# A two-layer hybrid trunk on one core: the scheduler plays the program through with another simulator of instruction times

## The chip, the core and the metric

The kernel runs on one core of a Trainium2 chip. The metric is the time of one execution in device microseconds (us); lower is better. TensorE (PE, with its weight load PEld), VectorE (DVE), ScalarE (ACT), GpSimd (POOL) and SyncE (SP, which issues the transfers here) each run their own stream of instructions in the order in which the program was laid down, and wait for one another on semaphores.

## The reference

512 prompt tokens and 8 x 4 decode tokens (N = 544) go through two layers, an mLSTM mixer and a gated DeltaNet (GDN) mixer, each followed by an MLP; every sub-layer ends in a LayerNorm. All is float32, D = 1024.

```python
for layer in range(DEPTH):                      # 0: mLSTM, 1: gated DeltaNet
    y, state = mixer[layer](x, state)           # projections, scan over the tokens, gate, output projection
    x = layer_norm(ALPHA * x + y)
    x = layer_norm(ALPHA * x + square(relu(x @ w1)) @ w2)

def step(S, xc):                                # the GDN scan, chunk after chunk
    u_c, w_c, attn_c, qg_c, kdec_c, gL_c = xc
    v_new = u_c - w_c @ S
    o = qg_c @ S + attn_c @ v_new
    S = gL_c * S + kdec_c.T @ v_new
    return S, o                                 # then o is normalised per head
```

The mLSTM scan is of the same kind (a state that each chunk reads and renews). The outputs are the tokens and all the states.

## The kernel before

**The products.** Activations stand as feature tiles, 128 features by 544 tokens, cut into two halves of 272. A float32 product is made of three matmuls of rounded parts (`mm3`, L157: hi hi, lo hi, hi lo). `load_w` (L143) brings a tile of weights in through SP's queue, ACT makes its high part (L110) and DVE its low part (L111). The L157 matmuls are most of PE's work; those of the projections depend on nothing but weights and the layer's input, so they can be done while PE would otherwise wait for something else. This is called filler below.

**The steps.** The mixers are written as steps in a fixed program order, `ORDER_A` for mLSTM and `ORDER` for GDN:

```python
ORDER_A = "p0 s0 p1 s1 d0 y0 p2 s2 p3 s3 w0 d1 y1 w1"
ORDER = "p0 a0 p1 i0 a1 d0 s0 p2 i1 u0 a2 s1 y0 p3 i2 a3 d1 s2 p4 i3 u1 s3 a4 w0 y1 p5 i4 p6 a5 d2 s4 w1 u2 i5 s5 y2 a6 p7 i6 a7 d3 s6 w2 u3 i7 s7 y3 w3"
```

`p` projects a unit (a quarter of mLSTM, an eighth of GDN), `a` prepares a GDN unit, `i` inverts its triangular blocks, `s` scans it over four chunks, `d` does the decode steps of a group, `u` renews the decode states, `y` projects and applies the output gate, `w` is the output projection. The steps `a`, `i`, `s`, `d` and `u` are written under `tc.high_priority(offset=HP)` with HP = 400 (L830, L833, L1374): the scheduler takes a ready instruction of these before a ready one of the rest.

**A scan is a chain.** One chunk of a GDN scan goes from engine to engine: PE L1180 (the state times k and q) → DVE L1183 (rhs, twice) → PE L1192 → DVE L1194 (vd) and ACT L1196 (vn) → PE L1200, with DVE L1203 renewing the state → PE L1210 → DVE L1212 (oi) → ACT L1152 twice, L1153, L1154 (the heads' norm) → DVE L1156 (go_on) → PE L1169 (transposes) → ACT L1171. Then the next chunk's L1180. The decode step of mLSTM goes PE L782 → ACT and DVE L672 to L683 (the norm, one small instruction after the other) → PE L785, then PE L795 against DVE L796. The update of the GDN decode states is PE L1327, three matmuls, against DVE L1332, four instructions, eight times a group. These chains work in PSUM tiles of tag s (`pm_s`, two banks), the projections in tag g (`pg_t`, three banks); one bank set can be used while the other waits.

**What fixes the order.** The program is written inside `tile.TileContext` (L1526). It collects the instructions, and its scheduler lays down one order per engine: it plays the program through with a model of how long each instruction takes, and whenever an engine is free there it gives it the ready instruction of the highest priority. Program order and `high_priority` give the priority; the model of times decides what is ready when. On the chip the order is fixed: an instruction that has to wait holds up everything behind it on its engine.

By time the stages lie so: mLSTM mixer to 284 us, MLP to 665, GDN mixer to 1440, MLP and the last LayerNorm to the end.

Of the kernel before, what the change touches and what calls it, by code (L numbers as in the profile page):

```python
# [16 lines left out]
P = 128  # L17
# [53 lines left out]
def hybrid_kernel(  # L71
# [46 lines left out]
    def gtile():  # L118
        """A bank for a product; the mlp has seven in turn."""
        tag = "g"  # L120
        if once:
            tag = once.pop(0)
        elif wide:
            wide.append(wide.pop(0))
            tag = wide[-1]
        if tag != "g":
            return mtile(tag)[:, :HN]
        return pg.tile([P, 512], F32, tag="g", name="pg_t", bufs=BANKS[0])[:, :HN]
# [7 lines left out]
    wn, wx = [0], [None]  # L136

    def load_w(src, alloc=None):
        """A tile of weights as hi and lo float32r parts."""
# [12 lines left out]
    def mm3(ps, h, wh, wl, xh, xl, first=True, last=True):  # L152
        """ps += W^T x for one half of the tokens: hi hi + hi lo + lo hi."""
# [11 lines left out]
    def gate_w(i, wt=None):  # L165
        """The gates' weights, side by side: hi in columns 0-47, lo in 64-111."""
# [9 lines left out]
    def gate_mm(ps, wt, h, k):  # L176
        """One half of the tokens: W_hi x on rows 0-47, W_lo x_hi on rows 64-111."""
# [4 lines left out]
    def projs(srcs, alloc=None, skip=2):  # L182
        """Feature tiles of the projections of X, the first half of the tokens first; alloc: of the weights after skip."""
# [46 lines left out]
    with tc.tile_pool(name="tmpc", bufs=1) as tp:  # L230
# [4 lines left out]
        # keep where t > s (strict) / t >= s  # L235
# [4 lines left out]
        # block of four: col // 4 == row // 4  # L240
# [5 lines left out]
        # rowm[r, j] = (r // 4 == j)  # L246
# [6 lines left out]
        # bmask[r, b] = (r % 32 // 4 == b)  # L253
# [3 lines left out]
        # bm16[r, j] = (r // 16 == j)  # L257
        G.affine_select(bm16, o1[:, :8], pattern=[[-16, 8]], compare_op=ALU.is_ge, fill=0.0, base=0, channel_multiplier=1)
        G.affine_select(bm16, bm16, pattern=[[16, 8]], compare_op=ALU.is_ge, fill=0.0, base=15, channel_multiplier=-1)
        # upper[r] = -(r // 16 is even)  # L260
        V.reduce_sum(upper, bm16[:, 0::2], axis=mybir.AxisListType.X, negate=True)
        # dmask[r, h] = (r % 32 == h)
# [6 lines left out]
        # hm[r, q, h] = (r == 64 q + h) + (r == 64 q + 32 + h)  # L269
        for q in range(2):  # L270
            V.tensor_tensor(hmr[:, q], ident[:, 64 * q:64 * q + HV], ident[:, 64 * q + 32:64 * q + 32 + HV], op=ALU.add)
        # lvl[i]: upper off-diagonal blocks at block size 2**i: same 2s block, row in its first half, col in its second
# [11 lines left out]
    class LayerNorm:  # L284
        """Post-norm of the residual in XR, by halves of the tokens; the sums are of x - c, c a mean of 128 features
        taken one stage before the residual is complete."""
# [72 lines left out]
    def out_proj(src, yh, yl, first, ln=None):  # L359
        """src [4, 128, 2, 4, 128]: output tiles in pairs, four contraction tiles each; ln: of the next stage."""  # L360
# [10 lines left out]
    def out_proj_ln(src, yh, yl, ln, alloc, nxt=None):  # L371
        """The last stage, one half of the tokens after the other, each followed by its layer norm."""
# [8 lines left out]
        for h in range(2):  # L381
            pss = []
            for j in range(KD):
                if j == 0 and h == 0:
                    # before the last contraction tile is there
# [68 lines left out]
    def softplus(tile, out, x, r):  # L454
        """out = softplus(x) on partitions r (log1p with its first-order correction)."""
# [6 lines left out]
        # u - (w - 1)  # L462
# [5 lines left out]
    def sigmoid_chain(t, src):  # L468
        """t = sigmoid(src), through exp and ln only; src None: t holds it, clamped."""
# [10 lines left out]
    def selector(pool, g, n):  # L480
        """float32r lhsT that pick head 4g + h's row (hi and lo) for n columns each."""
# [4 lines left out]
    def expand_rows(pool, src, g):  # L486
        """[rows, 32 sample columns] of the stack -> [rows, (head of four, 32)], each head's rows only."""
# [9 lines left out]
    def expand_rows_r(pool, src, g, n):  # L497
        """The same of n hi/lo pairs of row blocks, kept in float32r."""
# [10 lines left out]
    # ================= layer 0: mLSTM =================  # L509
    ln = LayerNorm(0)  # L510
    with tc.tile_pool(name="mc", bufs=1, reuse_waits="tile") as mc, ExitStack() as mx:
# [88 lines left out]
        # what is written late comes where the gates were, what the layer norm reads next to it  # L600
# [13 lines left out]
        def project(u):  # L614
            """q, k, v of a pair of heads (features of the two on partitions 0-63 and 64-127)."""
# [33 lines left out]
            # exp(b_t - m_t + i_s - b_s), s on partitions  # L649
# [880 lines left out]
```

## Time and profile before

| what | before |
|---|---|
| runs | 1839.61, 1844.43, 1849.94 us |
| median | 1844.43 us |
| profiled execution, its own time | 1839.61 us |
| its span, first to last instruction | 1839.6 us |
| instructions | 33677 |
| PE busy | 97% of the span |
| PE's weight load busy | 94% |
| DVE, ACT, POOL busy | 58%, 46%, 1% |
| mean granted TensorE clock | 0.979 of full |

The profiled execution is the fastest of the three runs. A PE that is 97% busy leaves 55 us of the span in which it runs nothing. The granted clock has two levels, 2.4 GHz (1.00) and 1.2 GHz (half); a mean of 0.979 over the span says that in a small part of it the clock was at the lower one.

### The profile page before, as it was taken

The numbers are of one execution on the slowest core, as the hardware profiler recorded it, in microseconds if no ns is written. First come the engines' busy times: TensorE is split into PE (matmuls) and PEld (weight loads), VectorE is DVE, ScalarE is ACT, GpSimd is POOL, SyncE is SP. The second block draws the span as 40 slices with busy tenths as digits, with TensorE's granted clock in tenths as the row PEclk, the third lists the DMA queues.
The fourth block names the chain that finished last, engine by engine and source line by source line (L and its number), as shares of the span: only waits on it lengthen the run. The fifth ranks groups of instructions, "written<-read, shape, count | busy, mean of one in ns | idle before, by whom it ended". The sixth has DMA issues, their size and how long they took to land.

```text
span 1839.6 us, 33677 instructions
## 1 busy us (share of the span) xinstructions
PE 1784.3 (97%) x13620; PEld 1720.3 (94%) x13620; DVE 1070.4 (58%) x2622; ACT 844.7 (46%) x1922; POOL 13.7 (1%) x32
## 2 busy tenths in 40 slices
PE   7999999999999999899999999999999999999997
PEld 6999998999999998898999999899998999999996
DVE  6464767432344377767748857875668643234436
ACT  6444356331243147665647456646446532124314
POOL 2000000000000000000000000000000000000000
PEclk9999998999999999899979999999899999999999
DMA  4132122223223222224221413331232232322311
GB/s 159 58 104 67 67 92 92 77 85 92 86 87 105 83 70 62 66 65 135 68 75 55 150 57 111 108 93 59 87 108 84 81 92 82 92 90 84 112 61 50
DMA packets 84284, 158.75 MB, mean 86 GB/s; under 512 B 37536, under 2 KB 41504, under 8 KB 83616
## 3 DMA queue, kind: packets, MB, share of 16 engines
q1 hardware_dynamic: 84128, 156.60, 27.8%
q8 instruction: 107, 1.75, 0.4%
q14 instruction: 49, 0.40, 0.1%
HBM read 140.51 MB, written 16.06 MB: 85 GB/s over the span
## 4 chain that ended last, share of the span: by engine, by line
PE 83%; DVE 8%; ACT 6%; DMA 2%; issue 1%; SPq 0%; ACTq 0%; DVEq 0%
PE pg_t L157 39%; PE pm_s L157 12%; PE pm_a L157 12%; PE pm_a L1110 4%; PE pm_s L1282 2%; PE pm_s L1180 1%; DVE lnt L341 1%; ACT wh L110 1%; DVE lnt L342 1%; PE pm_s L1200 1%; PE pm_s L1327 1%; PE pm_a L1050 1%; PE pm_s L1192 1%; PE pm_s L1210 1%; DVE wl L111 1%
## 5 line engine op out<-in xcount | busy, mean ns | idle before, releaser
L111 DVE TENSOR_TENSOR wl<-wraw,wh 128x1024 fp32r<-128x1024 f32 x200 | 244.7, 1223 | 370.0 <-ACT wh L110 369.7
L157 PE MATMUL pg_t<-XH,wh 128*128 128x272 f32 x1480 | 442.8, 299 | 9.1 <-ACT XH L110 8.2
L157 PE MATMUL pg_t<-XH,wl 128*128 128x272 f32 x1480 | 438.6, 297 | 0.5 <-DVE wl L111 0.5
L157 PE MATMUL pg_t<-XL,wh 128*128 128x272 f32 x1480 | 438.0, 296 | 0.0
L110 ACT CAST wh<-wraw 128x1024 fp32r<-128x1024 f32 (+1 forms) x201 | 210.3, 1046 | 476.1 <-PE pg_t L157 230.0
L157 PEld LDWEIGHTS pg_t<-XH,wh 128*128 128x128 f32 x1480 | 284.1, 192 | 12.3 <-ACT XH L110 8.2
L157 PEld LDWEIGHTS pg_t<-XL,wh 128*128 128x128 f32 x1480 | 284.0, 192 | 1.2
L157 PEld LDWEIGHTS pg_t<-XH,wl 128*128 128x128 f32 x1480 | 283.3, 192 | 1.7 <-DVE wl L111 0.7
L157 PE MATMUL pg_t<-h,wh 128*128 128x272 f32 x672 | 129.1, 289 | 0.0
L157 PEld LDWEIGHTS pg_t<-h,wh 128*128 128x128 f32 x672 | 105.6, 188 | 0.3
L157 PE MATMUL pg_t<-h,wl 128*128 128x272 f32 x336 | 96.8, 288 | 0.0
L157 PE MATMUL pm_a<-h,wh 128*128 128x272 f32 x496 | 95.3, 288 | 0.0
L157 PE MATMUL pm_s<-h,wh 128*128 128x272 f32 x496 | 95.0, 288 | 0.0
L157 PE MATMUL pm_s<-XH,wh 128*128 128x272 f32 x288 | 84.4, 293 | 0.0
L157 PE MATMUL pm_s<-XH,wl 128*128 128x272 f32 x288 | 83.9, 291 | 0.0
L157 PE MATMUL pm_s<-XL,wh 128*128 128x272 f32 x288 | 83.8, 291 | 0.0
L157 PE MATMUL pm_a<-XL,wh 128*128 128x272 f32 x280 | 82.0, 293 | 1.0 <-DVE XL L353 0.8
L157 PE MATMUL pm_a<-XH,wh 128*128 128x272 f32 x280 | 82.2, 293 | 0.0
L157 PE MATMUL pm_a<-XH,wl 128*128 128x272 f32 x280 | 81.0, 289 | 0.0
L357 DVE SCALAR_TENSOR_TENSOR XR<-XR,pg_t 128x272 f32<-128x272 f32 x118 | 50.7, 432 | 48.4 <-PE pg_t L157 48.2
L959 DVE SCALAR_TENSOR_TENSOR acc<-pre,cst,acc 128x568 f32<-128x568 f32 x96 | 77.0, 802 | 2.8 <-ACT acc L957 2.4
L157 PEld LDWEIGHTS pm_s<-h,wh 128*128 128x128 f32 x496 | 77.9, 188 | 0.2
(559 smaller groups left out, 3997.7 us busy)
## 6 DMA issues: line engine op xcount, KB each, us to landing
wraw<-in_w SPq DMA_DIRECT2D x64, 512.0 KB, 3.6
wraw<-in_wb SPq DMA_DIRECT2D x48, 512.0 KB, 3.7
wraw<-in_w2a SPq DMA_DIRECT2D x32, 512.0 KB, 3.6
sst<-in_s SPq DMA_DIRECT2D x64, 256.0 KB, 3.4
wraw<-in_wa SPq DMA_DIRECT2D x24, 512.0 KB, 3.7
wraw<-in_w2b SPq DMA_DIRECT2D x24, 512.0 KB, 3.6
out_ss<-sst SPq DMA_DIRECT2D x32, 256.0 KB, 2.7
wraw<-in_wbo SPq DMA_DIRECT2D x16, 512.0 KB, 3.5
```

The source lines that it names most:

```text
L110: S.copy(hi, src)
L111: V.tensor_tensor(lo, src, r32(hi), op=ALU.subtract)
L157: T.matmul(ps, lhsT=wt[:, k, :], rhs=xt[k][:, HS[h]], start=first and k == 0 and q == 0, stop=last and k == n - 1 and q == 2,)
L341: V.tensor_tensor(t, x, rs, op=ALU.mult)
L342: V.tensor_tensor(t, t, mu, op=ALU.subtract)
L357: V.scalar_tensor_tensor(x, x, ALPHA if first else 1.0, ps, op0=ALU.mult, op1=ALU.add)
L959: V.scalar_tensor_tensor(acc, pre[:, q:q + WC], cw[q], acc, op0=ALU.mult, op1=ALU.add)
L1050: T.matmul(pk[:, q * 256:(q + 1) * 256], lhsT=kq[:, 0, c0:c0 + P], rhs=kq[:, :, c0:c0 + P], start=True, stop=True)
L1110: T.matmul(ps[:, c], lhsT=left[:, c], rhs=right[:, c], start=True, stop=True)
L1180: T.matmul(pks[:, w], lhsT=kq[:, w, cc], rhs=St, start=True, stop=True)
L1192: T.matmul(pv[:, j], lhsT=X[:, 4 * (ch // 2) + 2 * j + ch % 2], rhs=rhs[:, j] if ch else vtok[:, j, 0], start=True, stop=True)
L1282: T.matmul(pkq[:, bb], lhsT=ts[bb // 4][:, bb % 4], rhs=kqf[:, :, o:o + 4], start=True, stop=True)
```

## The change

The context is opened with the flag that makes the scheduler play the program through with the simulator of instruction times instead of its default model. Nothing else that has an effect is changed: the other lines of the diff take comments and docstrings out.

```diff
-    with tile.TileContext(nc) as tc:
+    with tile.TileContext(nc, schedule_with_timeline_sim=True) as tc:
         hybrid_kernel(tc, *args)
...
     def gtile():
-        """A bank for a product; the mlp has seven in turn."""
+
         tag = "g"
```

The instructions are the same; their order on each engine is new. On PE 9639 lines differ, on DVE 3509, on ACT 2057, on SP 376, on POOL 38. The MLPs keep their order nearly as it was; the two mixers are shuffled throughout.

The first place is PE in the last scan of the GDN stage (`s7`). Names: `St` the state, `rhs`, `vd`, `vn` the chain's vectors, `go_on` the normed heads, `gyh`, `gyl` the gated output that the output projection reads; `XH`, `XL` with L157 are a projection. Before, from the end of one chunk's L1200 on:

```order
L1200 MATMUL pm_s<-vd,ktok 128x256
L157 MATMUL pg_t<-XH_80,wl 128x272
L1210 MATMUL pm_s<-vn,A 128x128 x2
L157 MATMUL pg_t<-XH_81,wh 128x272
L157 MATMUL pg_t<-XL_89,wh 128x272
L157 MATMUL pg_t<-XH_81,wl 128x272
L157 MATMUL pg_t<-XH_82,wh 128x272
L157 MATMUL pg_t<-XL_90,wh 128x272
L157 MATMUL pg_t<-XH_82,wl 128x272
```

More such rows follow, 32 in this case, up to the chunk's L1169. Now two of the chunks read:

```order
L1192 MATMUL pm_s<-rhs,X 128x128 x2
L1200 MATMUL pm_s<-vd,ktok 128x256
L1210 MATMUL pm_s<-vn,A 128x128 x2
L1169 MATMUL pm_s<-ident,go_on 128x128 x2
L1180 MATMUL pm_s<-St,kq 128x256 x2
L1192 MATMUL pm_s<-rhs,X 128x128 x2
L1200 MATMUL pm_s<-vd,ktok 128x256
L1210 MATMUL pm_s<-vn,A 128x128 x2
L1169 MATMUL pm_s<-ident,go_on 128x128 x2
L1180 MATMUL pm_s<-St,kq 128x256 x2
L1192 MATMUL pm_s<-rhs,X 128x128 x2
```

No filler is left between the links of these chunks. In the whole of scan 7 it now stands in three places: 20 L157 between the first chunk's L1180 and L1192, and two and four of them within the last chunk.

The second place is PE at the end of scan 1 and in the first decode step (`d0`) of the mLSTM stage. Names: `ho_hn` the normed heads, `KQX`, `QX`, `KX` the decode tokens' k and q, `cn` the decode states. Before:

```order
L779 MATMUL pm_s<-vr,sws 128x129
L782 MATMUL pm_s<-cn,QX 128x129 x16
L157 MATMUL pg_t<-XL_90,wh 128x272
L157 MATMUL pg_t<-XH_82,wl 128x272
L157 MATMUL pg_t<-XH_75,wh 128x272
L157 MATMUL pg_t<-XL_83,wh 128x272
L157 MATMUL pg_t<-XH_75,wl 128x272
```

These L157 go on, 25 in all, until L785 with `ho_hn`. Now:

```order
L696 MATMUL pm_s<-ident,ho_hn 128x128
L752 LDWEIGHTS identb
L752 MATMUL pm_s<-masks,identb 128x128
L753 MATMUL pm_s<-exprow_r,onesr 128x128
L758 MATMUL pm_s<-KQX_403 128x128 x2
L762 MATMUL pm_s<-ident,vsx 128x128
L764 MATMUL pm_s<-ident,KQX_403 128x128 x2
L779 MATMUL pm_s<-vr,sws 128x129
L782 MATMUL pm_s<-cn,QX 128x129 x16
L785 MATMUL pm_s<-ident,ho_hn 128x128
L795 MATMUL pm_s<-vr,KX 128x129 x6
L157 MATMUL pg_t<-XH_75,wh 128x272
```

The decode step runs from L747 to the sixth L795 without filler, and so do the last two chunks of scan 1 ahead of it (from L703 on). In the middle of the scans it went the other way: in the second chunk of scan 6, for one, 4 L157 stood between L1180 and L1192 before and 24 do now.

## Rows read from the trace of the kernel before

**Rows 1.** The page: span, busy time of each engine with its share and instructions.
```profile
span 1839.6 us, 33677 instructions
PE 1784.3 (97%) x13620; PEld 1720.3 (94%) x13620; DVE 1070.4 (58%) x2622; ACT 844.7 (46%) x1922; POOL 13.7 (1%) x32
```

**Rows 2.** The page: the chain that ended last, shares of the span by engine.
```profile
PE 83%; DVE 8%; ACT 6%; DMA 2%; issue 1%; SPq 0%; ACTq 0%; DVEq 0%
```

**Rows 3.** The waits of PE: line waited for: us in total, times, longest us.
```profile
PE pg_t L157 <- ACT XH L110: 8.2, 1, 8.2
...
PE pm_t L1001 <- DVE xb L1086: 3.6, 1, 3.6
PE pm_s L1169 <- DVE go_on L1156: 2.6, 2, 1.8
```

**Rows 4.** Windows: from:to, us, busy PE PEld DVE ACT POOL, PEclk, DMA, GB/s.
```profile
65.00:284.00 219.00, 216.13 (x1676) 207.33 (x1674) 131.87 (x358) 101.69 (x283) 0.23 (x2) 1.00 0.24 77
...
310.00:640.00 330.00, 330.00 (x2627) 329.62 (x2626) 124.47 (x154) 98.93 (x149) 0.00 (x0) 1.00 0.29 88
727.00:765.00 38.00, 29.80 (x187) 27.17 (x187) 29.00 (x99) 28.04 (x74) 0.00 (x0) 0.88 0.19 47
765.00:930.00 165.00, 159.88 (x1235) 147.76 (x1235) 118.06 (x373) 101.12 (x282) 0.00 (x0) 0.98 0.29 83
930.00:960.00 30.00, 29.96 (x169) 29.48 (x168) 10.76 (x31) 8.72 (x19) 0.00 (x0) 0.66 0.33 86
960.00:1290.00 330.00, 327.89 (x2545) 309.11 (x2544) 243.65 (x715) 193.29 (x508) 0.00 (x0) 1.00 0.30 91
1290.00:1312.00 22.00, 22.00 (x120) 21.51 (x119) 10.68 (x31) 6.84 (x15) 0.00 (x0) 0.61 0.45 129
...
1350.00:1403.00 53.00, 50.95 (x377) 46.21 (x376) 39.17 (x97) 30.51 (x76) 0.00 (x0) 1.00 0.43 138
```

**Rows 5.** The chain, three pieces of it: start us, us, engine, tile, line, count.
```profile
109.03 3.16 PE pg_t L157 x25
...
501.60 3.03 PE pg_t L157 x24
...
1378.16 4.02 PE pg_t L157 x32
```

**Rows 6.** Groups by line, a GDN chunk's DVE and ACT links: busy, mean ns, idle before.
```profile
L1183 DVE SCALAR_TENSOR_TENSOR rhs<-pm_s,colpb,vtokb 128x128 f32<-128x128 f32 x48 | 14.7, 344 | 6.1 <-PE pm_s L1180 6.0
...
L1194 DVE TENSOR_TENSOR vd<-pm_s,scl 128x256 f32<-128x256 f32 x32 | 13.5, 422 | 4.9 <-PE pm_s L1192 4.5
...
L1212 DVE TENSOR_TENSOR oi<-oi,pm_s 128x256 f32<-128x256 f32 x24 | 9.9, 414 | 0.5 <-PE pm_s L1210 0.4
...
L1152 ACT ACTIVATE go_sq<-oi 128x128 bf16<-128x128 f32 x48 | 14.4, 303 | 11.1 <-DVE oi L1212 11.1
...
L1152 ACT ACTIVATION_READ_ACCUMULATOR go_sq<-oi 128x1 f32 x48 | 9.1, 189 | 0.0
...
L1153 ACT ACTIVATE go_ss<-go_ss,eps_rms,nrm 128x2 f32<-128x2 f32 x32 | 12.3, 385 | 0.5
...
L1154 ACT ACTIVATE go_ss<-go_ss,nrm 128x2 f32<-128x2 f32 x32 | 9.3, 290 | 0.4
...
L1156 DVE TENSOR_TENSOR go_on<-oi,go_ss 128x256 f32<-128x256 f32 x24 | 10.1, 419 | 4.2 <-ACT go_ss L1154 4.2
```

**Rows 7.** The timeline at the end of the mLSTM decode's norm: start us, us, instruction.
```profile
111.79 0.29 DVE L683 TENSOR_TENSOR ho_hn<-pm_s,ho_d 128x128 f32<-128x128 f32 x1
...
112.23 0.30 PE L785 MATMUL pm_s<-ident,ho_hn 128*128 128x128 f32 x1
```

**Rows 8.** Groups by line: the update of the decode states, and L1180.
```profile
L1332 DVE SCALAR_TENSOR_TENSOR sst<-sst,glc,pm_s 128x128 f32<-128x128 f32 x128 | 35.9, 342 | 11.5 <-PE pm_s L1327 11.2
...
L1327 PE MATMUL pm_s<-VM,KM 128*128 128x512 f32 x96 | 29.8, 418 | 0.0
...
L1180 PE MATMUL pm_s<-St,kq 128*128 128x256 f32 x96 | 24.8, 381 | 0.0
```

## The prediction

> **What bounds the kernel now.** I read the page first, then the chain, PE's waits, and then windows stage by stage, since an average over mixers and MLPs says little. PE is busy 1784.3 us of 1839.6 [rows 1], so it runs nothing for 55.3 us, and it carries 83% of the chain that ended last [rows 2]. DVE and ACT have room on average. The waits of PE [rows 3] are few and mostly at stage borders: 8.2 us at the start for the first activations, 3.6 us at the start of GDN, and in the scans hardly any, 2.6 us in all for the normed heads. The windows [rows 4] show the same: an MLP leaves no idle at all (330.00 of 330.00 us), the mLSTM mixer 2.87 (219.00 - 216.13), the middle of GDN 5.12 and 2.11, the last scan 2.05 (53.00 - 50.95). The present order hides chains behind filler: 24 projection matmuls in a row take 3.03 us on the chain [rows 5], 0.126 each, and the 4.02 us of norm work between L1210 and L1169 of a late chunk are filled with 32 of them.
>
> What can a new order do, then? Nothing to PE's work; only to the idle time. Where fillers are put into a chain, idle goes; where they are taken out of one, it comes. So the sum is made of places.
>
> **Place 1, the end of GDN: filler taken out.** A chunk without filler makes PE wait three times. After L1192 for vd: 0.42 us. After L1210 for oi, two squares with their accumulator reads, L1153, L1154 and go_on: 0.41 + 2 x (0.30 + 0.19) + 0.39 + 0.29 + 0.42 = 2.49. After L1180 for the two rhs: 2 x 0.34 = 0.69 [rows 6]. With some 0.05 for each hand-over, my estimate from the gaps of such rows, that is 0.5, 2.6 and 0.75. By the new order of scan 7: chunk one 0.5 + 2.6 = 3.1; chunk two the same, since 20 fillers (2.5 us) stand in the wait for its rhs; chunk three 0.75 + 0.5 + 2.6 = 3.85; chunk four 0.75 + 0.25 + 2.1 = 3.1, two fillers covering half of its second wait and four some 0.5 of its third. Together 13.1 us. Scan 6's last two chunks have only the inverse's matmuls beside them, which wait for ACT themselves: 2 x 3.5 = 7, the 3.85 of a bare chunk less a little. The update stands alone too: eight groups, each three L1327 (29.8 us / 96 = 0.31 each, 0.93) against four L1332 (4 x 0.342 = 1.37) [rows 8], so DVE sets the pace, 8 x 0.44 = 3.5. The inverse's own last round trips, with nothing beside them, I put at 2. Sum 25.6; the 2.05 of idle that were there [rows 4] are in it, so **+23.5**. Its lower end is 11: only scan 7 less 2.05. The upper is 33, if ACT and DVE, which have the weights of the output projection to split at the same time, delay each link by half.
>
> **Place 2, end of scan 1 and decode 0: filler taken out.** The norm of the decode step took from 109.03, where the last L782 ended and filler began [rows 5], to 112.08 (111.79 + 0.29), and L785 could start at 112.23 [rows 7]: 3.05 us and a hand-over, covered by 25 fillers, 3.16 us. Without them it is 3.05 of idle. The same lines make the norm of a scan's chunk; there L723 and the next scores cover some 0.6, so 2.45 each for the last three, 7.3. The small steps from L747 to L779 I put at 1.3, the six L795 against DVE at 1. **+12.6**, between 6 (the norms of the scan half covered) and 16. Decode 1, ahead of the output projection, has its L785 bare too: 3.05 and 1 for L795, **+4**.
>
> **Place 3, GDN around scan 5, inverse 6 and decode 3.** In 35 us of PE's work DVE is now given 139 instructions where it had 61. At 243.65 / 715 = 0.34 us each [rows 4] that is 47 us, 12 more than PE's, and chunk three of scan 5 has no filler between its links. What DVE is given there it lacks later. Between 0 and +12, I take **+8**, since both a lone chunk and a busy DVE speak for the upper half.
>
> **What it wins.** In the middle of the scans the fillers per link grow. By PE busy at most 2.87 + 5.12 + 2.11 = 10.1 us can be won there [rows 4]. By the weight load it looks like more: idle 11.67 + 17.24 + 20.89 = 49.8. But a load takes 1720.3 / 13620 = 0.126 us [rows 1], and a matmul of L1327 0.31 and of L1180 24.8 / 96 = 0.26 [rows 8]: behind these the loader stands idle while PE works, 96 x 0.18 + 96 x 0.13 = 30 us of the 49.8. That leaves 19.3. Between 10.1 and 19.3 I take the middle, **-15**. The Trainium skill (Perfetto Trace Analysis, Identifying the Most-Contended Engine) says that matmul busy time is a poor measure, since pipelined matmuls look otherwise in a trace, and that the weight loads' busy share should be used: by that alone 49.8 us are to be had and the change would win. The trace agrees in the MLP, where both are full, and differs in the scans by those 30 us.
>
> **The clock.** In two stretches the granted clock fell towards 1.2 GHz although PE was busy: 0.66 in 930-960 and 0.61 in 1290-1312, which cost 0.34 x 30 = 10.2 and 0.39 x 22 = 8.6 us; in 727-765, where PE idled 8.2 us, it was 0.88, 4.6 us [rows 4]. Place 1 is a stretch of the last kind, longer. Bounds -18.8 (both falls go) and +20 (place 1, some 55 us, at 0.64 like the worst). I take the nearest row, **+5** for the waits of place 1, and leave the two falls where they are. The Trainium skill (TensorE: Matmul & The Clock Gate, HAM oscillation) says that waits between bursts of matmuls let the clock fall back, so the bursts start slow: it speaks against this change at place 1. The trace agrees at 727-765 and not at 930-960, where PE was busy 29.96 of 30 us.
>
> **Queues.** On SP weight loads move ahead of state stores and state loads. DMA carries 2% of the chain [rows 2]; what hides it is the one tile of weights that is always loaded ahead. If a load came late PE would wait for a split, which it does nearly nowhere now. POOL has 13.7 us in all. Both at nothing.
>
> **The sum.** 23.5 + 12.6 + 4 + 8 - 15 + 5 = +38. The profiled execution is itself the fastest run, 1839.6 us; so 1877, against a median of 1844.4 **+1.8%**. A measurement of this kernel tells some 0.5%, 9 us, from no change: same is 1835 to 1854.
>
> **Rivals.**
> *The fillers win more than the bare chains cost.* Then the idle of the weight loader was real waiting, too short for a list of waits: -49.8 in place of -15, and the two falls of the clock, which belong to the old order, go: -18.8 in place of +5. 1839.6 + 48.1 - 49.8 - 18.8 = 1819. It decides as soon as more than 48 us are won. For it: the loader's rows; against it: the matmuls of L1327 and L1180 explain 30 of them, and an order that had room for 50 us would show waits in the list, which has a few in each stage. Chance 0.15.
> *It evens out.* The 19.3 are all won and the two falls of the clock go, the bare chains cost what I say: 1839.6 + 48.1 - 19.3 - 18.8 = 1850. Chance 0.12. That the change does nothing at all (the flag ignored) is excluded by PE's order, of which 9639 lines differ; 0.01.
> *The clock falls for the whole of the bare end* and the links are delayed by DVE's and ACT's splits: 1877 + 15 for the clock (20 in place of 5) + 9.5 (33 in place of 23.5) = 1901. For it: 0.61 in a stretch that had no idle at all. Against it: 0.98 to 1.00 around. Chance 0.2.
> *My sum* as it stands, with its bounds about 1855 to 1892: 0.52.
>
> **How the numbers follow.** Forecast 1877. The likeliest case alone is 1855 to 1892; the range goes down to the even case and a little of the first, and up past the slow clock: 1835 to 1908, with some 0.15 below it and 0.05 above. Faster by over 0.5%: 0.15. Within: the even case, the ignored flag and a corner of the sum, 0.14. Slower: 0.71.
>
> **What would show it.** Right, if the window of scan 7 has PE idle some 3 us a chunk, and waits of L1169 for go_on of about 2.5 us each appear in PE's list where 2.6 in all stood; if L785 waits 3 us for ho_hn twice; if the middle of the scans has less idle than 10 us; if the MLP windows are unchanged. Place 3 is right if waits there end with DVE. Wrong, if PE's busy time changes by more than the clock explains, if L1169 shows no waits (then the order has cover that I missed), or if 930-960 and 1290-1312 have lost their low clock and with it more than the bare chains cost.

## The result, and the profile after

The changed kernel takes 1951.22 us, the median of four runs (1945.08 to 1954.73), where the kernel before took 1842.02 on the same chip: a ratio of 1.0595 with a 95% interval of 1.0543 to 1.0646. It is slower by some 109 us. The prediction had 1877, slower by 38, with a range that ended at 1908. The sign was right and the size nearly three times too small.

The page of the changed kernel, its span and busy times, which answer to [rows 1], and then its chain's shares by engine, to [rows 2]:

```profile
span 1953.0 us, 33633 instructions
PE 1822.9 (93%) x13620; PEld 1761.5 (90%) x13620; DVE 1082.3 (55%) x2622; ACT 849.1 (43%) x1922; POOL 15.8 (1%) x32
```

```profile
PE 82%; DVE 9%; ACT 4%; DMA 3%; issue 1%; SPq 0%; ACTq 0%; DVEq 0%
```

PE has the same 13620 matmuls. It is idle for 1953.0 - 1822.9 = 130.1 us where it was 55.3, so +74.8; and it is busy for 1822.9 - 1784.3 = 38.6 us more, for the same work. Both together are the 113.4 us between the two profiled spans (the medians are 109 apart). For the second part the clock is enough: the mean granted clock went from 0.979 to 0.948, so the two spans fall short of full clock by some 39 us (0.021 x 1839.6) and some 102 (0.052 x 1953.0), 63 more, part of it while PE waits.

PE's waits in the changed kernel (line waited for: us in total, times, longest), which answer to [rows 3]:

```profile
PE pm_t L1001 <- DVE kq L963: 18.3, 4, 10.2
PE pm_s L1169 <- DVE go_on L1156: 15.8, 7, 4.5
PE pg_t L157 <- ACT XH L110: 7.4, 1, 7.4
PE pm_a L157 <- ACT XH L352: 7.0, 2, 4.6
...
PE pm_s L785 <- DVE ho_hn L683: 4.5, 2, 2.3
```

The second and the last row are the bare chains of the forecast. The first and the fourth are waits that it did not have at all.

To see where the time came from I cut both traces at the same counts of PE matmuls, where both orders have done the same number of matmuls, though not always the same ones. Windows of the kernel before (from:to, us, busy PE PEld DVE ACT POOL with counts, PEclk, DMA share, GB/s): mLSTM mixer; its last decode step, output projection and LayerNorm; start of GDN; its middle; place 3; end of GDN with its LayerNorm (place 1):

```profile
54.80:268.90 214.10, 212.25 (x1653) 203.89 (x1652) 124.79 (x345) 95.49 (x283) 0.23 (x2) 1.00 0.25 81
268.90:319.80 50.90, 48.17 (x303) 43.70 (x302) 37.03 (x85) 32.69 (x63) 0.00 (x0) 0.90 0.27 82
...
702.40:814.10 111.70, 102.40 (x752) 96.42 (x751) 79.41 (x247) 75.81 (x195) 0.96 (x1) 0.92 0.22 63
814.10:1238.10 424.00, 417.17 (x3152) 391.30 (x3152) 312.01 (x946) 241.77 (x650) 0.00 (x0) 0.98 0.32 93
1238.10:1294.00 55.90, 55.72 (x453) 52.98 (x451) 32.77 (x85) 35.88 (x83) 0.00 (x0) 1.00 0.20 61
...
1381.80:1449.90 68.10, 62.49 (x452) 58.41 (x451) 55.19 (x135) 43.62 (x95) 0.00 (x0) 1.00 0.29 87
```

The same six windows of the changed kernel:

```profile
57.80:289.40 231.60, 219.08 (x1653) 212.58 (x1652) 126.34 (x346) 94.13 (x285) 0.22 (x2) 0.96 0.22 71
289.40:351.20 61.80, 48.28 (x302) 44.50 (x302) 40.19 (x92) 35.17 (x68) 0.00 (x0) 0.89 0.24 83
...
734.50:860.60 126.10, 104.70 (x753) 101.65 (x751) 83.09 (x256) 80.34 (x197) 0.95 (x1) 0.85 0.20 55
860.60:1288.60 428.00, 416.33 (x3153) 397.27 (x3152) 298.48 (x875) 238.50 (x617) 0.00 (x0) 0.95 0.30 86
1288.60:1366.50 77.90, 68.43 (x452) 61.13 (x451) 53.37 (x169) 41.61 (x118) 0.00 (x0) 0.89 0.25 76
...
1449.10:1561.20 112.10, 83.31 (x451) 72.58 (x452) 66.47 (x170) 46.92 (x116) 0.00 (x0) 0.80 0.22 73
```

Read each pair twice, for its length and for what of it is idle (length less PE busy). For the windows between these I worked out the same: the first 55 us grew by 3.0, the two MLPs by 0.7 and 2.1, and the stretch between place 3 and place 1 lost 5.2.

| stretch | longer by | of it idle | of it PE busy | forecast |
|---|---|---|---|---|
| mLSTM mixer (place 2) | 17.5 | 10.7 | 6.8 | 12.6 |
| decode 1, projection, LayerNorm | 10.9 | 10.8 | 0.1 | 4 |
| start of GDN | 14.4 | 12.1 | 2.3 | none |
| middle, and the stretch ahead of place 1 | -1.2 | 5.9 | -7.1 | -15 |
| place 3 | 22.0 | 9.3 | 12.7 | 8 |
| end of GDN and LayerNorm (place 1) | 44.0 | 23.2 | 20.8 | 23.5, +5 for the clock |
| start and MLPs | 5.8 | 2.8 | 3.0 | 0 |
| sum | 113.4 | 74.8 | 38.6 | 38 |

Two cautions go with this table. Falls of the clock come and go between executions of one order: e1 below, which has the order of before, takes 117.2 us at the start of GDN (clock 0.87) and 416.7 in its middle (1.00), where the profile of before has 111.7 (0.92) and 424.0 (0.98). And the column of PE busy is not the clock alone. What the clock can take in a stretch is at most (1 - PEclk) of its length: 22.4 us at place 1 and 9.3 in the mLSTM mixer, more than the column has, but 8.6 at place 3, less than its 12.7. In the middle it is up to 21.4 (0.05 x 428.0); without that PE would be busy there for some 395 us, where e1 at full clock is busy for 409.7:

```profile
817.10:1233.80 416.70, 409.67 (x3153) 383.62 (x3152) 311.95 (x946) 241.67 (x650) 0.00 (x0) 1.00 0.33 94
```

So in the middle the new order won up to about 15 us, by this estimate, as busy time of PE and not as idle; the clock took it back.

Inside place 1 the chain shows one bare chunk from its normed heads to the next ones. Chain of the changed kernel (start us, us, engine, tile, line, count):

```profile
1485.42 0.66 PE pm_s L1169 x2
1486.08 1.72 PE pm_s L1180 x4
1487.82 0.36 DVE rhs L1183
...
1488.32 1.21 PE pm_s L1192 x4
1489.55 0.44 DVE vd L1194
1490.03 1.22 PE pm_s L1200 x2
1491.25 0.87 PE pm_s L1210 x4
1492.14 0.43 DVE oi L1212
1492.59 0.70 ACT go_sq L1152 x4
1493.32 0.40 ACT go_ss L1153
1493.74 0.30 ACT go_ss L1154
1494.07 0.44 DVE go_on L1156
...
1494.64 0.66 PE pm_s L1169 x2
```

It takes 9.22 us. From the end of L1210, 1492.12, to L1169 PE waits 2.52 us; the forecast had 2.6 from [rows 6]. But L1180 takes 1.72 us here, and 0.86 in the chain of the kernel before, half the speed: over this chunk the granted clock is 0.50, so the links themselves run at 1.2 GHz. Not every wait does it. One chunk earlier, where 20 fillers stand ahead, L1200 ran at full clock right behind its wait for `vd`, in 0.71 us in place of 1.22. The chain of the kernel before, and then that of the changed kernel:

```profile
1382.43 0.86 PE pm_s L1180 x4
```

```profile
1481.66 0.71 PE pm_s L1200 x2
```

The 10.2 us of the first wait lie at the start of GDN. The row of PE, then the chain that leads to it:

```profile
806.00 1.12 PE L1001 MATMUL pm_t<-ident,kq 128*128 128x128 f32 x4 [10.17 <-DVE kq L963]
```

```profile
790.15 0.33 DVE A L1068
...
791.47 1.53 DMA dg<-U
793.15 2.59 DMA ub<-dg
795.76 0.18 DVE tb L1084
...
797.99 0.80 DVE acc L959
...
805.25 0.70 DVE kq L963
```

The inverse of a unit sends a matrix to memory and back (`dg<-U`, `ub<-dg`). DVE's next instruction is L1084, which takes it up, and behind it in DVE's order stand the convolutions of the next unit (L959), whose result `kq` PE waits for with its own projections queued behind L1001. The transfer itself is not what fills PE's wait: L1084 began at 795.76, and PE's wait at 795.83 (806.00 less 10.17). What fills it is the way from there to `kq`, DVE's convolutions between the small steps of the inverse and ACT's steps behind them. How much earlier `kq` would come if DVE had not waited before that was not tried. DVE does wait longer for such transfers in the changed kernel:

```profile
DVE tb L1084 <- DMA ub<-dg: 10.3, 5, 5.3
DVE X L1101 <- DMA xc<-dx: 8.6, 5, 3.7
```

In the kernel before, L1084 and L1101 waited 3.2 us in all for them.

### The profile page after: what moved, and what is told of

It is laid out like the page before. It is cut to its first block, busy times and chain, and to the rows that moved or that the text cites. A ratio compares the mean times of both kernels' runs of the same rounds, so it can differ in the third digit from the quotient of the medians.

```text
span 1953.0 us, 33633 instructions
## 1 busy us (share of the span) xinstructions
PE 1822.9 (93%) x13620; PEld 1761.5 (90%) x13620; DVE 1082.3 (55%) x2622; ACT 849.1 (43%) x1922; POOL 15.8 (1%) x32
## 4 chain that ended last, share of the span: by engine, by line
PE 82%; DVE 9%; ACT 4%; DMA 3%; issue 1%; SPq 0%; ACTq 0%; DVEq 0%
PE pg_t L157 41%; PE pm_s L157 12%; PE pm_a L157 12%; PE pm_a L1110 3%; PE pm_s L1282 2%; PE pm_s L1180 1%; DVE wl L111 1%; PE pm_t L317 1%; PE pm_a L1050 1%; DVE lnt L341 1%; DMA out_ss<-sst 1%; PE pm_a L1131 1%; PE pm_s L1200 1%; PE pm_s L1327 1%; DVE acc L959 1%
## 5 line engine op out<-in xcount | busy, mean ns | idle before, releaser
L157 PE MATMUL pg_t<-XH,wh 128*128 128x272 f32 x1480 | 446.8, 302 | 19.7 <-ACT XH L110 7.4
L157 PE MATMUL pg_t<-XH,wl 128*128 128x272 f32 x1480 | 442.1, 299 | 2.6 <-DVE wl L111 2.6
L157 PE MATMUL pg_t<-XL,wh 128*128 128x272 f32 x1480 | 440.0, 297 | 2.9 <-DVE XL L111 1.9
L157 PEld LDWEIGHTS pg_t<-XH,wh 128*128 128x128 f32 x1480 | 288.8, 195 | 23.9 <-ACT wh L110 7.9
L157 PEld LDWEIGHTS pg_t<-XL,wh 128*128 128x128 f32 x1480 | 288.7, 195 | 4.5 <-DVE XL L111 2.3
L157 PEld LDWEIGHTS pg_t<-XH,wl 128*128 128x128 f32 x1480 | 287.7, 194 | 4.3 <-DVE wl L111 3.4
L157 PE MATMUL pg_t<-h,wh 128*128 128x272 f32 x672 | 128.7, 288 | 0.0
L157 PEld LDWEIGHTS pg_t<-h,wh 128*128 128x128 f32 x672 | 105.6, 188 | 0.2
L157 PE MATMUL pg_t<-h,wl 128*128 128x272 f32 x336 | 96.9, 288 | 0.0
L157 PE MATMUL pm_a<-h,wh 128*128 128x272 f32 x496 | 94.4, 287 | 0.0
L157 PE MATMUL pm_s<-h,wh 128*128 128x272 f32 x496 | 94.3, 287 | 0.0
L157 PE MATMUL pm_a<-XH,wh 128*128 128x272 f32 x280 | 83.4, 298 | 8.2 <-ACT XH L352 7.0
L157 PE MATMUL pm_a<-XL,wh 128*128 128x272 f32 x280 | 83.5, 298 | 0.6 <-DVE XL L353 0.3
L157 PE MATMUL pm_s<-XH,wh 128*128 128x272 f32 x288 | 83.9, 291 | 0.0
L157 PE MATMUL pm_s<-XH,wl 128*128 128x272 f32 x288 | 83.5, 290 | 0.0
L157 PE MATMUL pm_s<-XL,wh 128*128 128x272 f32 x288 | 83.5, 290 | 0.0
L157 PE MATMUL pm_a<-XH,wl 128*128 128x272 f32 x280 | 82.4, 294 | 0.0
L959 DVE SCALAR_TENSOR_TENSOR acc<-pre,cst,acc 128x568 f32<-128x568 f32 x96 | 76.7, 802 | 3.4 <-ACT acc L957 2.4
L157 PEld LDWEIGHTS pm_a<-h,wh 128*128 128x128 f32 x496 | 77.8, 188 | 0.0
```

What stands on the lines that cost most here:

```text
L157: T.matmul(ps, lhsT=wt[:, k, :], rhs=xt[k][:, HS[h]], start=first and k == 0 and q == 0, stop=last and k == n - 1 and q == 2,)
L959: V.scalar_tensor_tensor(acc, pre[:, q:q + WC], cw[q], acc, op0=ALU.mult, op1=ALU.add)
```

## The experiments

Two theories stood at the start. The first is that of the prediction, with the clock priced higher: PE's order takes the fillers out of the chains, and that is the loss. The rival is that the new orders of DVE and ACT cost time of their own, PE's only part of it.

Nearly all runs use one tool. A table of instruction numbers fixes, for a chosen set of instructions of chosen engines, the order in which they stand; it adds issue order alone, no waits. With every instruction of every engine in it, one kernel's order is reproduced under the other's scheduler.

```diff
+def pinned(tc, nc):
+    here = {i.name: i for i in nc.cur_bb.bb.instructions}
+    for table in TABLE:
+        at, prev = 0, None
+        for step in table:
+            at += step
+            i = here.get(f"I-{at}")
...
+            if prev is not None:
+                tc.add_manual_dep(i, prev.name, mybir.DependencyInfo(mybir.DependencyClass.NoSync, mybir.DependencyReason.DATA), reason="pinned")
+            prev = i
...
         hybrid_kernel(tc, *args)
+        pinned(tc, nc)
```

Each of these runs is the changed kernel or the kernel before with this diff and another table; a sentence gives what is in the table. What is not in it, the run's own scheduler lays out anew round what is: in e2, for one, DVE's order comes out nearer to that of the kernel before than to that of the changed kernel. Differences in us are differences of ratios times 1842.

### Is it the order alone, and whose fault is it

**e1**: the changed kernel, everything in the order of before. 

> The changed kernel, with the order of every engine pinned to that of the kernel before (a table of instruction numbers; order of issue alone, no waits). If the change acts through the order alone: 1842 us, the kernel before. If the flag also changes something else (waits, buffers), it stays above 1855.

Measured 1835.19 us, ratio 0.9983 (0.9956 to 1.001). The order on the engines is all of the change, as far as that interval tells.

**e16**: the changed kernel with another reach of the priorities.

```diff
-HP = 400
+HP = 4000
```

> The changed kernel with the offset of the high-priority steps raised from 400 to 4000. If the chains' matmuls stand late because projections rank before them: shorter covers, 1880 to 1920. If the times of the play-through decide when a chain's matmul counts as ready, whatever its rank: the same covers (13 to 23 projection matmuls a link, a third of the chunks bare) and 1935 to 1965.

1944.83 us, 1.0582 (1.0549 to 1.0616), as without it. Pushing the chains' steps further ahead in priority does not bring the fillers back to their waits (L1169 still waits for `go_on` seven times, 14.1 us in all). That leaves the times by which the program is played through, which the flag changes; it is an argument, and which of those times is off was not found.

### Which places

**e4**: the changed kernel, all engines put back in the last decode step, scans 6 and 7 and the output projection behind them. 

> Only the last steps of the GDN stage (decode 3, scan 6, output 2, update 3, inverse 7, scan 7, gate and output 3) and the LayerNorm behind them pinned to the order of before, on all engines. In the profile of the changed kernel these cost 34.6 + 8.5 us more than before. If the stretch is a loss of its own: 1951 - 43 = 1908. If its idle only moves (the stages before hand over later): 1930 or more. The low clock in it (34 us at half) goes with it if the clock follows PE's waits.

1924.44 us, 1.0479 (1.0451 to 1.0506): 21 us back. Its window of place 1 reads as in the kernel before, length, idle and clock:

```profile
1464.00:1532.00 68.00, 62.71 (x452) 58.41 (x451) 55.17 (x134) 43.44 (x94) 0.00 (x0) 1.00 0.29 87
```

So 44 us came back here, and the whole profiled span is 27.9 us shorter than that of the changed kernel. Some 12 us were lost just ahead, in the stretch before this window (95 by 83); the rest is a few us elsewhere. That the old end counts on fillers which the new order had used up is my reading of it, not shown.

**e10**: the other way round, the kernel before with the new order of all engines at the end of GDN alone. 

> The old scheduler, with the end of GDN (from decode 3 on, and the LayerNorm behind it) pinned to the order of the changed kernel on all engines: place 1 of the prediction alone. By the trace of the changed kernel 43 us: 1837 + 43 = 1880. If place 1 is only worth what I forecast for it (23.5 and 5 for the clock): 1866. If most of its loss was carried in from the stages ahead: under 1855.

1881.95 us, 1.0222 (1.0168 to 1.0275): +41. Its window of place 1, and then L1169 in PE's waits:

```profile
1382.00:1494.50 112.50, 84.64 (x447) 73.75 (x446) 65.71 (x169) 47.69 (x118) 0.00 (x0) 0.79 0.22 73
```

```profile
PE pm_s L1169 <- DVE go_on L1156: 12.8, 5, 4.0
```

Everything of place 1, the 112 us, the clock of 0.8 and the waits, comes with this piece of order and needs nothing else of the change.

**e15**: the same with PE's instructions alone. 

> The old scheduler, with only PE pinned to the order of the changed kernel, and only at the end of GDN; the others' orders are the old scheduler's. On all engines the same stretch cost 45 us (1882). If the chains without filler on PE are the whole of place 1: 1875 to 1885 again. If DVE's and ACT's orders hold part of it: 1850 to 1870. If orders that don't belong together cost more: 1890 or above.

1885.90 us, 1.026 (1.0221 to 1.0299): +48, not told apart from e10. At place 1 it is PE's order, as the prediction said: the fillers are taken out.

**e7**: the changed kernel, all engines put back in the mLSTM mixer and the LayerNorm behind it. 

> Only the mLSTM mixer with its LayerNorm and the first products behind it pinned to the order of before, on all engines. By the trace of the changed kernel the stretch costs 31 us more than before. If the losses of the stages are separate: 1951 - 31 = 1920, GDN's loss unchanged at about 80. If the gain is taken back later as in the tail's run (44 won, 17 given back ahead of the seam): 1930 to 1945.

1909.51 us, 1.0385 (1.0351 to 1.0418): 39 back, where the windows of the mixer and the LayerNorm give 28.4 and the first stretch 3.0. The intervals of the two kernels are wider than that difference.

**e11**: the kernel before with PE's new order in the mLSTM mixer alone. 

> The old scheduler, with PE's order alone pinned to that of the changed kernel, and only in the mLSTM mixer with its LayerNorm; the others' orders are the old scheduler's. In the changed kernel the stretch costs 31 us. If PE's order does it (place 2, the bare decode norms): 1837 + 17 to 31 = 1854 to 1868. If DVE's and ACT's orders do most of it: 1840 to 1850.

1871.73 us, 1.0179 (1.0151 to 1.0208): +33, a little above the 17 to 31 expected. Here too PE's order alone is enough for the loss.

**e17**: the changed kernel with the start of GDN put back. 

> The changed kernel, with all engines put back to the order of before among the instructions written from the first projection of GDN to the preparation of its third unit; the rest stays new. By the windows the start of GDN is longer by 14.4 us than before and the middle by 4.0. Place account: the 14 come back and nothing else changes, some 1937 us, 1.052. Orders as a set: like the end of GDN, where 44 us came back in their stretch and 16 were lost ahead of the seam, part is lost again at the border, where the projections of this part are then used up otherwise than the next part counts on: 1942 to 1950. If it comes to 1925 or less, the start also sets what follows it.

1929.92 us, 1.0472 (1.0432 to 1.0512): 23 back, more than the 14 of its window. The wait of 10.2 us is gone from PE's list and PE's idle in this window falls to 8.7 us, where the kernel before had 9.3. The window itself is shorter by 3.5 us only, at a low clock (the old order had 0.92 in the profile of before, 0.87 in e1, 0.84 in e15):

```profile
734.20:856.80 122.60, 113.88 (x751) 108.13 (x750) 79.40 (x247) 75.80 (x195) 0.95 (x1) 0.82 0.21 57
```

In this profile, the slowest of the four runs, more came back behind the window: 4 us in the middle and 6.5 in place 3, which the table does not hold.

**e18**: the changed kernel with the middle of GDN and place 3 put back. 

> The changed kernel, with all engines put back among the instructions written from the preparation of GDN's third unit to the last decode step, which holds place 3. By the windows middle, place 3 and the next stretch are together longer by 4.0 + 22.0 - 5.2 = 20.8 us than before. Place account: 1930 us, 1.048. Orders as a set: part of it is lost at two borders, 1935 to 1950. With the mixer of mLSTM (-42) and the end of GDN (-27) put back each alone, the four parts would make -104 by the place account, against -113 for all of them together; a sum well short of that says that the borders, where an old and a new order meet, cost time of their own.

1932.50 us, 1.0484 (1.0452 to 1.0517): 20 back, as the windows say in sum, but not in their parts: place 3 and the stretch behind it are 30 us shorter than in the changed kernel, and the middle, with its old order, is 8 longer (435.9 by 428.0). Place 3 is again a stretch without idle and at full clock:

```profile
1291.50:1348.50 57.00, 56.82 (x462) 54.48 (x461) 32.01 (x77) 33.37 (x77) 0.00 (x0) 1.00 0.19 57
```

The four parts give 39 + 23 + 20 + 21 = 103 us, against 113 for all of them together (1.0595 - 0.9983). The gap is smaller than the uncertainty of the sum: the interval of the changed kernel (some 9 us to either side) enters it four times and the whole only once, some 28 us. That the sums agree so well is then partly luck, and e4, e17 and e18 show that time put back at one place can come back or be lost at another. A place that costs its own time, with nothing else of the change, is shown for the end of GDN (e10, e15) and the mLSTM mixer (e11); for the start and the middle of GDN it is not.

### Which engine

**e2**: the changed kernel with PE's order put back, the others left to the new scheduler. 

> Only PE's order pinned to that of before; the other engines' orders are left to the new scheduler. Theory A (PE's fillers taken out of the chains are the loss): close to 1842, at most 1860. Theory B (DVE and ACT get orders in which what PE needs next stands behind work that waits): most of the loss stays, about 1900 to 1940, with PE's waits for L963 and for the LayerNorm still there.

1927.74 us, 1.0497 (1.0473 to 1.0521). Only 18 of 113 us come back. Place 1 has no bare chain any more (of L1169's waits 1.6 us lie there), but other waits have come. PE's:

```profile
PE pm_t L317 <- ACT lnt L313: 21.2, 9, 5.3
PE pm_s L1169 <- DVE go_on L1156: 13.3, 14, 2.7
PE pm_t L1001 <- DVE kq L963: 11.4, 3, 6.4
```

**e3**: DVE and ACT put back, PE left to the new scheduler. 

> Only the orders of DVE and ACT pinned to those of before; PE's order is left to the new scheduler. Theory A: still about 1920 to 1950, since the bare chains stay in PE's order. Theory B: about 1850 to 1880, and PE's waits for L963 (18.3 us) go.

2026.76 us, 1.1037 (1.1011 to 1.1064): worse than either kernel, which no theory had expected. PE's order is not that of the changed kernel either.

**e5**: PE and DVE put back. 

> The orders of PE and DVE pinned to those of before, ACT, POOL and SP left to the new scheduler. With PE alone pinned it was 1928 us. If DVE's order is what held PE up there (pieces that wait for a transfer put ahead of what PE needs: L963, go_on): 1840 to 1855. If ACT's or SP's order does it as well: 1870 to 1910.

1867.28 us, 1.0152 (1.0117 to 1.0187).

**e6**: PE and ACT put back. 

> The orders of PE and ACT pinned to those of before, DVE, POOL and SP left to the new scheduler. If DVE's order is what holds PE up: still 1900 to 1930, with DVE waiting for ub<-dg some 10 to 15 us. If ACT's order (the first link of most chains back to PE) does it: 1840 to 1870.

1911.08 us, 1.0385 (1.0344 to 1.0426).

**e9**: the kernel before with PE's new order in the whole program. 

> The other way round: the old scheduler, with only PE's order pinned to that of the changed kernel; DVE, ACT, POOL and SP get the orders that the old scheduler finds for it. If PE's order (chains without filler, matmuls put where the new scheduler thought them ready) holds most of the loss: 1920 to 1950. If the new orders of DVE and ACT hold most of it: 1860 to 1890, the bare chains alone.

1986.81 us, 1.0804 (1.0765 to 1.0843), slower than the changed kernel, which has other orders of the other engines to go with it.

**e14**: as e2, with DVE's instructions of the projections and of the preparation of units in the old order among themselves. 

> PE's order pinned to that of before, and of DVE only the GDN projection's and prepare's instructions (convolution, L963 to L1027, and the inverse of the diagonal blocks, which waits for transfers) pinned among themselves. With PE alone pinned it was 1928, with PE and all of DVE 1867. If the order within this part is what held PE up (L1001 waiting for L963, DVE waiting for ub<-dg): 1875 to 1895. If it is DVE's order of this part against the chains' links and the LayerNorm: 1915 to 1930.

1912.68 us, 1.0418 (1.0399 to 1.0438): 15 us less than e2, far from the 64 that all of DVE's order gives (e2 to e5). DVE's share is not in that group alone.

With PE back, DVE's order is worth 64 us (e2 to e5), ACT's 21 (e2 to e6), and what is left in e5, ACT's with SP's and POOL's, 31 (e5 to e1). An order of one engine is good or bad only beside the others' orders: PE's alone costs 148 in e9, and to undo it alone gives 18 in e2. Each of these numbers holds for the orders that were found round the fixed ones; none is the share of an engine in the 113 us of the changed kernel, which stays open.

**e13**: the changed kernel with PE's scan links moved ahead, so that each has behind it about the number of projections that the kernel before has. 

> The changed kernel, with PE's order pinned to its own but for the scans' links: a matmul of a scan that stands behind more than 6 (L1192), 7 (L1200), 23 (L1169, L696) or 8 (L718) projection matmuls that come later in the program is moved ahead to that many, about the covers of the kernel before. The other engines' orders are left to the new scheduler. If late links on PE are what stretches the scans (42 us a scan against 27) and so empties the end: scans of 30 to 36 us and 1900 to 1935. If not: 1945 to 1960.

1971.14 us, 1.0739 (1.0707 to 1.077): slower. The theory was that the new order issues the links too late: in the trace of the changed kernel a link's operand lies ready some 2 us (median of 32 chunks, 1.9 for `go_on`, 1.8 for `vd`) before PE takes it, against 0.2 to 0.4 before. The delays went for the links L1192 and L1200 (0.3 us for either), for `go_on` half of it stayed (1.2), and the time rose. Late links at L1192 and L1200 are not the cause by themselves; for L1169 the run does not say.

### The clock

**e12**: the changed kernel, all orders kept, with 14 matmuls that nobody reads behind each chunk's L1210 of scan 7, where PE waits.

```diff
+                if u == 7:
+                    pw = mtile("t")[:, 0:P]
+                    for _ in range(14):
+                        T.matmul(pw, lhsT=ident, rhs=ident, start=True, stop=True)
```

> The changed kernel with all orders as they are, and 14 matmuls of 128x128 whose result nobody reads on PE behind each L1210 of the last scan, where PE waits for go_on. In the changed kernel the clock was at half for about 20 us from there on. If the waits let the clock fall: these falls go, 5 to 10 us less (1941 to 1946 against 1951). If the clock falls anyway, the idle matmuls take longer than the wait, and it is the same or up to 5 us more.

1946.20 us, 1.0588 (1.0552 to 1.0624): in the whole time it cannot be told from the changed kernel. The windows of scan 7 do tell. The changed kernel, then e12, and behind it two rows of e12's chain (start us, us, engine, tile, line, count; each of the 14 matmuls leaves two records):

```profile
1471.00:1504.30 33.30, 21.71 (x88) 17.19 (x89) 12.98 (x34) 9.27 (x35) 0.00 (x0) 0.69 0.13 44
```

```profile
1463.00:1492.70 29.70, 26.23 (x199) 24.14 (x200) 12.83 (x34) 9.27 (x35) 0.00 (x0) 1.00 0.16 50
```

```profile
1477.76 0.88 PE pm_s L1180 x4
...
1481.50 3.13 PE pm_t L1214 x28
```

With the waits filled the clock stays at 1.00, L1180 takes 0.88 us in place of 1.72, and the scan 3.6 us less, although each filling takes 3.13 us and so outlasts the wait of 2.5. This is not one execution's chance: the clock of scan 7 is 0.65 to 0.74 in all nine profiles with PE's new chunks there (the changed kernel, e7, e9, e10, e13, e15 to e18) and 1.00 in the nine where PE has the old ones (the kernel before, e1, e2, e4, e5, e6, e8, e11, e14); e3, with a third order of PE, has 0.89. That the low clock in scan 7 follows from PE's waits is shown; what it costs there is at least these 3.6 us.

**e8**: the kernel before, with the other kind of fall that the prediction left where it was, 930 to 960 us. There PE is busy, with runs of narrow matmuls, L1282, 128x8. They are put in groups of four with six projections between.

```diff
-L1282 MATMUL pm_s<-kqx,sst 128x8 x5
+L1282 MATMUL pm_s<-kqx,sst 128x8 x4
+L157 MATMUL pg_t<-XH_75,wh 128x272
+L157 MATMUL pg_t<-XL_83,wh 128x272
...
```

> The kernel before (old scheduler) with one change on PE: in decode 1 of GDN the 32 small matmuls L1282 (128x8) stand in groups of four with six projections between, where groups of 5, 11, 4, 4, 4, 4 stood with 4 to 15 between. In before the granted clock fell to half for 20.5 us there although PE was busy. Theory C (the clock falls where many matmuls of few columns follow each other, busy or not): the fall goes, about 9 us less, 1827 against 1837. Theory D (the fall comes from something else, or at random): no change.

1835.39 us, 0.9991 (0.997 to 1.0012): no gain. The window of the kernel before, of e8, and of e1, which has the very order of the kernel before:

```profile
926.00:960.00 34.00, 33.96 (x198) 33.21 (x198) 12.82 (x41) 11.85 (x30) 0.00 (x0) 0.70 0.29 76
```

```profile
926.00:960.00 34.00, 33.96 (x271) 32.58 (x271) 20.11 (x67) 17.45 (x41) 0.00 (x0) 1.00 0.39 104
```

```profile
926.00:960.00 34.00, 33.95 (x261) 32.48 (x259) 18.02 (x59) 15.92 (x39) 0.00 (x0) 0.95 0.36 102
```

The fall is gone in e8, but in e1 it is nearly gone with nothing changed. One execution has it and another has not, so the run settles nothing.

No version is measurably faster than the kernel before: e1 and e8 lie within 0.3% of it, the rest above.

## Why the prediction was wrong in size

The profiles are 113.4 us apart where the forecast had 38. Of the 75.3 us that it lacks, 33.6 are in the term of the clock and 41.7 in idle time: 20.9 in the middle of the scans, 12.1 at the start of GDN, 6.8 in the stretch with decode 1, and little elsewhere.

**The mechanism held at places 1 and 2.** The forecast went by places where fillers are put into a chain or taken out of one, e15 and e11 show that PE's order alone does it there, and two of the named waits appeared: L1169 after L1210 waits 2.52 us (2.6 forecast), L785 waits for `ho_hn` twice, 2.3 us each (3.05). The MLPs are unchanged. PE's idle at place 1 grew by 23.2 us where +23.5 was said; some 8 us of waits there are the LayerNorm's, which the forecast had not counted, so the agreement is partly luck. In place 3 most of PE's waits end with DVE (7 of 9 us), as it said.

**The step that failed first** is the sentence "Nothing to PE's work; only to the idle time", and with it the clock's term. PE's busy time grew by 38.6 us for the same matmuls: where a chain is bare PE runs links at half clock. I had the clock at +5, for place 1 alone, with +20 as the upper bound. At place 1 alone PE's busy time grew by 20.8 (clock 0.80; the bound was worked out from 0.64, called the worst row, where [rows 4] have 0.61 and 0.66). The mixer has 6.8 at 0.96, and place 3 12.7, of which its 0.89 explains at most 8.6. The row that I scaled from, 727 to 765 us with 0.88 [rows 4], is a stretch with 8.2 us of waits in 38; scan 7 waits in each of its chunks, 11.6 us in 33, and ran at 0.69. This term was short by 33.6 us. The Trainium skill (TensorE: Matmul & The Clock Gate, HAM oscillation) says that bursts after waits start slow; e12 agrees, since the filled waits leave the clock at 1.00. I cited it and priced it too low. The rival "the clock falls for the whole of the bare end" had this, with 15 for it, and stopped at one place.

**The second** is the win of 15 us in the middle of the scans. In idle time it did not come: idle grew by 4.8 us in the middle and by 1.1 in the stretch behind it, 20.9 us away from -15. I read the fillers per link of PE and took it that more of them cover more; but the largest waits in the middle are L1001's for `kq`, 5.7 us, which is no link of a scan. Something like the win came in PE's busy time, up to about 15 us by the estimate under the table, which the sum held for fixed, and the lower clock took it back.

**The third** is that I looked at one engine's order. "Queues ... Both at nothing" and the absence of any term for the start of GDN (14.4 us between the profiles, and 23 by e17) come from there: I held DVE's and ACT's orders for the same as before and counted only what PE's order did to them. They had 3509 and 2057 rows of difference. L1001 waits 18.3 us for `kq`, which DVE, at the longest of these waits, makes between the steps of the inverse. I had read the transfers off the chain, 2% of it [rows 2]; DVE now waits longer for those of the inverse, but ahead of the longest of PE's waits and not in it, so what they cost is not shown. Experiment e2 says how large the other engines' part can be: with PE's order of before, and the others as the new scheduler then lays them, 1.0497 - 0.9983, 95 us, are still lost.

**Sizes of the other terms.** Place 2 was 17.5 for 12.6 and the stretch with decode 1 was 10.9 for 4: the first has the clock in it, the second waits of the LayerNorm (L157 for `XH` of L352, 4.6 of the 7.0 us in PE's list, is the longest) that no term had. Place 3 was 22.0 for 8, more than half of it PE's busy time.

**The case against.** The prediction gave 0.15 to a win of 49.8 us by the weight load's idle time, which is what the Trainium skill (Perfetto Trace Analysis, Identifying the Most-Contended Engine) points to. The whole did not win. But the middle of GDN has 417.17 - 391.30 = 25.9 us between PE's and the loader's busy time before and 19.1 after, and by the estimate above PE's busy time at full clock fell with it: there was room that idle time does not show. The objection from [rows 8], that long matmuls leave the loader nothing to do, is weaker than I put it: only 72 of the 96 L1327 and of the 96 L1180 stand in the three windows, so they explain 23 of the 49.8, not 30, and the bound of 19.3 should have been 27. The two falls of the clock, which the low rivals let go with the old order, belong to no order: e1 has the old one and all but lacks the first.

**What stays open**: which of the modelled times moves the links and the waits; which engine's order makes the loss at the start and in the middle of GDN; and whether DVE with its convolutions ahead of L1084 would shorten the wait of L1001 by itself, which was not tried.

## What to carry to other kernels

When a schedule changes, compare the orders of all engines, not of the busiest alone: of 113 us PE's old order alone gave back 18. Price a bare chain at its waits and also at its own matmuls run at half clock; here PE's busy time grew by 38.6 us beside 74.8 of idle. Compare PE's busy time at equal clock, or a fall hides what an order wins. To find where a schedule loses, put the order back place by place, and also bring the new order of one place into the old kernel, which is the cleaner test (e10, e15). The places add up to 103 of 113 us, within a wide uncertainty; the engines do not add up, and the old orders of DVE and ACT with PE's left to the new scheduler made things worse (1.1037).

## What was not expected of the hardware

The granted clock fell where PE was busy nearly all the time as well as behind waits, and not in every execution: 926 to 960 us had 0.70 in one profile of the old order and 0.95 in another (e1), with 198 and 261 matmuls done in the same 34 us. A profiled stretch of low clock without idle is therefore no price that a change can be promised. And the clock answered within a scan: with matmuls that nobody reads in PE's waits it was 1.00 through a chain that otherwise had 0.65 to 0.74 on the mean.
